# Moving the value spreads, the table load and the last store in a transfer-bound softmax kernel

## The chip, the cores and the metric

The kernel runs on one core of a Trainium2 chip. The metric is the time of one execution on the device, in microseconds (us), and a kernel's figure is the median of its runs. Ratios are the mean time of one kernel's runs over the mean of the other's runs of the same rounds, with a 95% interval, so they are not quite the ratio of the medians quoted beside them.

A trace gives the *span*, which is 1.7 to 2.4 us shorter than the run's time. Engines are PE (matrix products), PEld (its weight loads), DVE (vector), ACT (scalar), POOL and SP. A "q" behind an engine's name (SPq, ACTq) is its instruction queue. Here SP issues every load and store.

## The reference

```python
def setup_inputs():
    scores = np.random.randn(8, 12, 1024, 1024).astype(np.float32)
    v      = np.random.randn(8, 12, 1024, 64).astype(np.float32)

def reference(scores, v):
    attn = np.exp(scores - np.max(scores, axis=-1, keepdims=True))
    attn = attn / (np.sum(attn, axis=-1, keepdims=True) + 1e-8)
    return np.matmul(attn, v).astype(np.float32)
```

Seen by the kernel, these are 96 independent heads, each with 4.194 MB of scores, 0.262 MB of values and 0.262 MB of output.

## The kernel before

A loop of 24 passes takes four heads each. For a head, ACT takes the exponential of 8 rows of scores in four instructions. (A "row" is one of a head's eight tiles of 128 x 1024 scores.) PE transposes a row in eight blocks, DVE copies the transposed row out of PSUM, and PE multiplies it with `vones`, the head's values beside a column of ones whose product is the row's sum. DVE then takes the reciprocal and multiplies (the normalisation). Below, *the last product* is the last of these multiplications on DVE, not one on PE. The maximum isn't subtracted, since the scores are small.

The values of four heads come as one block of 1.049 MB, and POOL casts them to half precision. DVE then *spreads* them, in four copies a head, from their compact layout into `vones`. A store carries two heads (0.524 MB).

```python
def heads(n0):
    for k in range(AHEAD):                      # four heads of a pass
        if k == 0:
            for s in range(S):
                spread_v(k, s)                  # head 0: its own values, at the start
        st = dict(vones=vones_bufs[k])
        for r in range(R):                      # 8 rows
            ...                                 # exp (ACT), 8 transposes (PE)
            copy = nc.vector.tensor_copy(out=pt[:], in_=psT[:])
            if k < AHEAD - 1 and r % (R // S) == 0:
                spread_v(k + 1, r // (R // S), copy)   # the next head's values
            if r == R - 1:
                load_next(k, n0)                # heads 0 and 1 of the next pass
            pending.append((n0, k, r, pt, st))
            if len(pending) > LAG:
                finish(pending.pop(0))          # products, normalise, store of heads 0 and 1
    while pending:
        finish(pending.pop(0))
    cast_v()                                    # POOL: the next pass's four heads of values
    last(n0)

def last(n0):
    before = queued[-1:]
    with tc.If(n0 < BH - 2 * AHEAD) as cmp:
        ...                                     # loads of heads 2 and 3, values, store
    with cmp.Else():
        with tc.If(n0 < BH - AHEAD) as cmp2:
            ...
            load(AHEAD - 2, BH - 2, (4, 4))     # the very last heads come in pieces
            load(AHEAD - 1, BH - 1, (4,))
            store(n0, AHEAD - T)
            load(AHEAD - 1, BH - 1, (2, 1, 1), 4)
        with cmp2.Else():
            ...
            store(n0, AHEAD - T)                # the very last store, whole
```

Of the kernel before, what the change touches and what calls it, by code (L numbers as in the profile page):

```python
# [9 lines left out]
FP16 = mybir.dt.float16  # L10
EXP = mybir.ActivationFunctionType.Exp
# [3 lines left out]
def kernel(  # L15
# [7 lines left out]
    P = 128  # L23
# [52 lines left out]
    def buffers(pool, count, shape, dtype, name):  # L76
        return [pool.tile(shape, dtype, name=f"{name}{k}") for k in range(count)]

    s_bufs = buffers(sb_pool, AHEAD, [P, R, SK], FP32, "s_nat")
    v_sb = sb_pool.tile([P, C // L, S, L, D], FP32, name="v_sb")  # L80
    v_half = sb_pool.tile([P, C // L, S, L, D], FP16, name="v_half")
    p_bufs = buffers(sb_pool, 8, [P, EB, SK], FP16, "p_nat")
    pt_bufs = buffers(sb_pool, 4, [P, SK], FP16, "pt")
    out_bufs = buffers(sb_pool, 2, [P, T, R, D], FP32, "out_sb")
# [16 lines left out]
    def after(a, b):  # L101

        tc.add_manual_dep(
            a.ins,
            b.ins.name,
            mybir.DependencyInfo(mybir.DependencyClass.NoSync, mybir.DependencyReason.DATA),
            reason="order",
        )

    def queue(dma):  # L110

        if queued:
            after(dma, queued[-1])
        queued.append(dma)
# [21 lines left out]
    def finish(u):  # L136

        n0, k, r, pt, st = u
        b, g = r // G, r % G
        if r == 0:  # L140
            st["recip"] = take(rc_bufs)
            st["out_sb"] = out_bufs[k // T]
        bank = psO_whole[:, b] if k % 2 == 0 else psO_banks[b][:, 0]
        for c in range(C):
            nc.tensor.matmul(  # L145
                out=bank[:, g * M : (g + 1) * M],
                lhsT=pt[:, c * P : (c + 1) * P],
                rhs=st["vones"][:, c, 0:M],
                start=(c == 0),
                stop=(c == C - 1),  # L150
            )
        if k % 2 == 1:
            if g == G - 1:
                normalise(k, st, b, b + 1)
        elif r == R - 1:
            normalise(k, st, 0, R // G)
        if r == R - 1 and k == T - 1:
            store(n0, 0)

    def store(n0, k):  # L160

        rows = out_bh.rearrange("(m x) y -> m x y", x=P)
        dma = nc.sync.dma_start(
            out=rows[bass.ds((n0 + k) // T, 1)].rearrange("o x y -> (o x) y"),
            in_=out_bufs[k // T][:].rearrange("x t r d -> x (t r d)"),
        )
        for other in stores:
            apart(dma, other)
            apart(other, dma)
        apart(dma, dma)  # L170
        stores.append(dma)
        queue(dma)

    stores = []

    def apart(dma, other):
        tc.declare_no_dep(
            dma.ins, other.ins, across_iterations=True, reason="stores of two heads are disjoint"
        )
# [12 lines left out]
    def load_v(n):  # L192

        rows = v_bh.rearrange("(m x) y -> m x y", x=P)
        queue(
            nc.sync.dma_start(  # L196
                out=v_sb[:].rearrange("x h s l d -> x (h s l d)"),
                in_=rows[bass.ds(n // AHEAD, 1)].rearrange("o x y -> (o x) y"),
            )
        )  # L200

    def cast_v():
        nc.gpsimd.tensor_copy(out=v_half[:], in_=v_sb[:])  # L203

    def spread_v(k, s, behind=None):

        copy = nc.vector.tensor_copy(  # L207
            out=vones_bufs[k][s * Q : (s + 1) * Q, :, 0:D].rearrange(
                "i (h l) d -> i h l d", l=L
            ),  # L210
            in_=v_half[k * Q : (k + 1) * Q, :, s],
        )
        if behind is not None:
            after(copy, behind)
# [6 lines left out]
# [6 lines that stand above are left out]
            queued[:] = before  # L227
            load(AHEAD - 2, (n0 + (2 * AHEAD - 2)) % BH)
            load_v((n0 + 2 * AHEAD) % BH)
            load(AHEAD - 1, (n0 + (2 * AHEAD - 1)) % BH)  # L230
# [3 lines that stand above are left out]
                queued[:] = before  # L234
                load(AHEAD - 2, BH - 2, (4, 4))
                load(AHEAD - 1, BH - 1, (4,))
                store(n0, AHEAD - T)
                load(AHEAD - 1, BH - 1, (2, 1, 1), 4)
            with cmp2.Else():
                queued[:] = before  # L240
                store(n0, AHEAD - T)

    def heads(n0):

        for k in range(AHEAD):
            if k == 0:
                for s in range(S):
                    spread_v(k, s)
            st = dict(vones=vones_bufs[k])
            for r in range(R):  # L250
                if r % EB == 0:
                    p_nat = take(p_bufs)
                    rows = 1 if k == AHEAD - 1 and r == R - EB else EB
                    for g in range(0, EB, rows):
                        nc.scalar.activation(  # L255
                            out=p_nat[:, g : g + rows, :].rearrange(
                                "p r (x v) -> p x r v", v=Q * L
                            ),
                            in_=s_bufs[k][:, r + g : r + g + rows, :].rearrange(
                                "p r (i x l) -> p x (r i) l", i=Q, l=L  # L260
                            ),
                            func=EXP,
                        )
                p_row = p_nat[:, r % EB, :].rearrange("p (h q l) -> p h l q", q=P, l=L)
                psT = take(psT_bufs)
                for c in range(C):
                    nc.tensor.transpose(  # L267
                        out=psT[:, c * P : (c + 1) * P],
                        in_=p_row[:, c // L, c % L, :],
                        identity=order16[:],  # L270
                    )
                pt = take(pt_bufs)
                copy = nc.vector.tensor_copy(out=pt[:], in_=psT[:])  # L273
                if k < AHEAD - 1 and r % (R // S) == 0:
                    spread_v(k + 1, r // (R // S), copy)
                if r == R - 1:
                    load_next(k, n0)
                pending.append((n0, k, r, pt, st))
                if len(pending) > LAG:
                    finish(pending.pop(0))  # L280
        while pending:
            finish(pending.pop(0))
        cast_v()
        last(n0)

    assert BH % AHEAD == 0 and BH >= 2 * AHEAD and SK == Q * S * C
    load_v(0)
    for k in range(AHEAD):
        load(k, k)
    cast_v()  # L290
    load_v(AHEAD)
    with tc.For_i(0, BH, AHEAD, iteration_sync="reg_based") as n0:  # L292
        queued.clear()
# [31 lines left out]
```

## Time and profile before

| | before |
|---|---|
| time, median of the first 3 runs (range) | 1066.09 us (1065.76 to 1066.24) |
| span of the profiled run | 1064.0 us |
| busiest engine over the span | DVE, 74% |
| DMA queue busy | 99.2% of the span |
| mean pass (2 to 16), moved bytes per second | 43.67 us, 432 GB/s |
| last head: first exp to end of the last product | 13.23 us |
| end of the last product to the end | 4.81 us |

The prediction below shows the lines that carry this reading. Three more groups of the page are the ones that the change moves: the table load, the spreads and the cast. The columns are busy us, mean ns of one, and, behind the second bar, the idle time of the engine just before them and what ended most of it.

```profile
L255 ACT ACT_TABLE_LOAD x24 | 30.8, 1283 | 89.8 <-DMA s_nat<-in_scores_dram 81.7
L207 DVE COPY vones<-v_half 32x512 f16<-32x512 f16 x384 | 109.4, 285 | 22.8 <-POOL v_half L203 6.0
L203 POOL CAST v_half<-v_sb 128x2048 f16<-128x2048 f32 x25 | 47.4, 1896 | 1002.3 <-DVE vones L207 957.1
```

ACT idles 89.8 us ahead of its table loads, nearly all of it until scores land. So a table load starts only when the scores are there and stands between their landing and the exp. POOL's cast waits for DVE's spreads, as it overwrites what they read. One pass on ACT's timeline (start, duration, group, and the idle time before it):

```profile
758.44 1.28 ACT L255 ACT_TABLE_LOAD   x1 [3.56 <-DMA s_nat<-in_scores_dram]
759.73 7.32 ACT L255 ACTIVATE p_nat<-s_nat 128x2048 f16<-128x2048 f32 x4
768.12 7.32 ACT L255 ACTIVATE p_nat<-s_nat 128x2048 f16<-128x2048 f32 x4 [1.07 <-SPq L226]
779.03 7.32 ACT L255 ACTIVATE p_nat<-s_nat 128x2048 f16<-128x2048 f32 x4 [3.58 <-DMA s_nat<-in_scores_dram]
```

A head's exps take 7.32 us and its landing interval is about 10.9 us, so ACT idles more than 3 us a head. The table load of 1.28 us is paid from that idle time.

### The profile page before, as it was taken

How to read it: one execution, taken by the hardware profiler on the slowest of the kernel's cores; microseconds unless marked ns; L12 is line 12 of the kernel's file. 1: busy time of each engine (PE TensorE's matmuls, PEld its weight loads, DVE VectorE, ACT ScalarE, POOL GpSimd, SP SyncE). 2: the span in 40 equal slices, each digit the busy share in tenths (PEclk: the TensorE clock that was granted, in tenths of full speed). 3: DMA queues.
4: the chain of work that ended last, by engine and by line, in shares of the span. 5: the costliest groups of instructions: out<-in, count | busy, mean ns of one | idle time of the engine just before them, and what ended most of it. 6: DMA issues, size and time to landing. Idle time of an engine off the chain costs nothing.

```text
span 1064.0 us, 32161 instructions
## 1 busy us (share of the span) xinstructions
PE 731.4 (69%) x12288; PEld 678.4 (64%) x12288; DVE 786.6 (74%) x1589; ACT 735.6 (69%) x432; POOL 48.1 (5%) x31
## 2 busy tenths in 40 slices
PE   2766766767766677677686776867666777666676
PEld 2665756667666667666575665767565666666675
DVE  3776876868768777677786776868768687687777
ACT  3766776666767668586676866667766668676685
POOL 0000000000000000000000000000000000000000
PEclk9888888878889888888988888888889788898989
DMA  9999999999999999999999999999999999999995
GB/s 397 431 418 434 426 433 434 433 434 432 432 434 432 425 443 430 429 431 428 433 431 436 432 434 434 431 434 424 441 427 434 432 426 435 432 432 428 440 425 236
DMA packets 24772, 453.06 MB, mean 426 GB/s; under 512 B 2752, under 2 KB 2752, under 8 KB 9152
## 3 DMA queue, kind: packets, MB, share of 16 engines
q1 hardware_dynamic: 24768, 453.00, 99.2%
q8 instruction: 4, 0.07, 0.0%
HBM read 436.21 MB, written 25.17 MB: 434 GB/s over the span
## 4 chain that ended last, share of the span: by engine, by line
DMA 81%; ACT 12%; issue 3%; ACTq 1%; PE 1%; DVE 0%; SPq 0%; PEld 0%; DVEq 0%
DMA s_nat<-in_scores_dram 81%; ACT p_nat L255 12%; PE psT L267 1%; ACTq L255 1%; ACTq L226 0%; ACTq L292 0%; PE psO L145 0%; DVE pt L273 0%; PE psO_whole L145 0%; SPq L184 0%; PEld L267 0%; ACTq L320 0%; DVE out_sb L129 0%; SPq L196 0%; PEld L145 0%
## 5 line engine op out<-in xcount | busy, mean ns | idle before, releaser
L255 ACT ACTIVATE p_nat<-s_nat 128x2048 f16<-128x2048 f32 (+1 forms) x408 | 704.8, 1799 | 228.1 <-DMA s_nat<-in_scores_dram 202.2
L267 PE MATMUL psT<-order,p_nat 128*128 128x128 f16 x6144 | 574.9, 246 | 269.9 <-ACT p_nat L255 263.9
L273 DVE COPY pt<-psT 128x1024 f16<-128x1024 f16 x768 | 515.8, 687 | 200.6 <-PE L267 109.4
L267 PEld LDWEIGHTS <-p_nat 128*128 128x128 f16 x6144 | 446.5, 123 | 298.3 <-ACT p_nat L255 295.7
L145 PEld LDWEIGHTS <-pt 128*128 128x128 f16 x6144 | 302.9, 107 | 81.0 <-DVE pt L273 77.7
L145 PE MATMUL psO<-vones,pt 128*128 128x65 f16 x3072 | 177.4, 201 | 53.9 <-DVE pt L273 50.2
L145 PE MATMUL psO_whole<-vones,pt 128*128 128x65 f16 x3072 | 189.9, 211 | 2.7 <-DVE pt L273 2.4
L207 DVE COPY vones<-v_half 32x512 f16<-32x512 f16 x384 | 109.4, 285 | 22.8 <-POOL v_half L203 6.0
L255 ACT ACT_TABLE_LOAD x24 | 30.8, 1283 | 89.8 <-DMA s_nat<-in_scores_dram 81.7
L203 POOL CAST v_half<-v_sb 128x2048 f16<-128x2048 f32 x25 | 47.4, 1896 | 1002.3 <-DVE vones L207 957.1
L129 DVE TENSOR_TENSOR out_sb<-psO,recip 64x256 f32<-64x256 f32 x192 | 81.1, 423 | 6.1
L129 DVE TENSOR_TENSOR out_sb<-psO_whole,recip 64x512 f32<-64x512 f32 x96 | 66.1, 688 | 3.0
L124 DVE RECIPROCAL recip<-psO 128x4 f32<-128x4 f32 x96 | 17.1, 178 | 34.4 <-PE psO L145 17.6
L124 DVE RECIPROCAL recip<-psO_whole 128x8 f32<-128x8 f32 x48 | 9.7, 203 | 4.5 <-PE psT L267 3.9
L71 DVE MEMSET vones<- 128x16 f16 x4 | 0.2, 72 | 0.8 <-PEq L309 0.8
L62 DVE CAST order<-ident 128x128 f16<-128x128 f32 x1 | 0.2, 227 | 0.4 <-POOL ident masks.py:199 0.4
masks.py:199 POOL TENSOR_SCALAR_AFFINE_SELECT ident<-ident 128x128 f32<-128x128 f32 x1 | 0.3, 295 | 0.1
masks.py:197 POOL MEMSET ident<- 128x128 f32 x1 | 0.2, 205 | 0.3 <-POOLq L309 0.3
L309 POOL MEMSET const-float32-0.0<- 128x1 f32 x1 | 0.1, 100 | 0.2 <-issue 0.2
L309 POOL MEMSET const-bfloat16-1.0<- 128x1 bf16 x1 | 0.1, 103 | 0.0
L309 POOL MEMSET const-uint8-127<- 128x1 uint8 x1 | 0.1, 103 | 0.0
L309 POOL MEMSET const-float32-1.0<- 128x1 f32 x1 | 0.1, 100 | 0.0
## 6 DMA issues: line engine op xcount, KB each, us to landing
s_nat<-in_scores_dram SPq DMA_DIRECT2D x96, 4096.0 KB, 35.8
v_sb<-in_v_dram SPq DMA_DIRECT2D x24, 1024.0 KB, 33.1
out_dram<-out_sb SPq DMA_DIRECT2D x48, 512.0 KB, 26.9
s_nat<-in_scores_dram SPq DMA_DIRECT2D x3, 2048.0 KB, 32.4
s_nat<-in_scores_dram SPq DMA_DIRECT2D x1, 1024.0 KB, 25.4
s_nat<-in_scores_dram SPq DMA_DIRECT2D x2, 512.0 KB
```

The source lines that it names most:

```text
L62: nc.vector.tensor_copy(out=order16[:].rearrange("p (t j) -> p t j", t=T), in_=ident32[:].rearrange("p (j t) -> p t j", t=T),)
L71: nc.vector.memset(vo[:, :, D : D + 2], 1.0)
L124: nc.vector.reciprocal(out=recip, in_=psO[:, :, :, D : D + 1])
L129: nc.vector.tensor_tensor(out=rows.rearrange("j (b g) d -> j b g d", g=G), in0=psO[part, :, :, 0:D], in1=recip[part].to_broadcast([W, last ...
L145: nc.tensor.matmul(out=bank[:, g * M : (g + 1) * M], lhsT=pt[:, c * P : (c + 1) * P], rhs=st["vones"][:, c, 0:M], start=(c == 0), stop=(c ...
L203: nc.gpsimd.tensor_copy(out=v_half[:], in_=v_sb[:])
L207: copy = nc.vector.tensor_copy(out=vones_bufs[k][s * Q : (s + 1) * Q, :, 0:D].rearrange("i (h l) d -> i h l d", l=L), in_=v_half[k * Q : ( ...
L255: nc.scalar.activation(out=p_nat[:, g : g + rows, :].rearrange("p r (x v) -> p x r v", v=Q * L), in_=s_bufs[k][:, r + g : r + g + rows, :] ...
L267: nc.tensor.transpose(out=psT[:, c * P : (c + 1) * P], in_=p_row[:, c // L, c % L, :], identity=order16[:],)
L273: copy = nc.vector.tensor_copy(out=pt[:], in_=psT[:])
L309: nc = _bacc.Bacc("TRN2", target_bir_lowering=False, num_devices=1)
```

## The change

It has three parts. The spreads of heads 2 and 3 go among the copies of heads 0 and 1. Those of the *next* pass's heads 0 and 1 stand in a branch ahead of the last head, skipped in the last pass; the cast moves forward to make that possible. A dummy exp ahead of heads 0 and 3 lets the table be loaded in idle time. The very last store goes out in two halves.

```diff
-    def store(n0, k):
+    def store(n0, k, parts=1):
...                                  # one issue for each part of T * R * D columns
-                store(n0, AHEAD - T)
+                store(n0, AHEAD - T, T)
...
-            if k == 0:
-                for s in range(S):
-                    spread_v(k, s)
+            if k == AHEAD - 1:
+                with tc.If(n0 < BH - AHEAD):
+                    for part in range(2 * S):
+                        spread_v(part // S, part % S)
+            if k % (AHEAD - 1) == 0:
+                table = nc.scalar.activation(out=spare[:], in_=order16[:, 0:1], func=EXP)
...
+                        if k % (AHEAD - 1) == 0 and r == g == 0:
+                            after(exp, table)
...
-                if k < AHEAD - 1 and r % (R // S) == 0:
-                    spread_v(k + 1, r // (R // S), copy)
+                if k < 2 and r % 2 == 0:
+                    spread_v(k + 2, r // 2, copy)
...
+            if k == 1:
+                cast_v()
         while pending:
             finish(pending.pop(0))
-        cast_v()
         last(n0)
...                                  # ahead of the loop, heads 0 and 1 are spread once
```

More of the change, by code (lines that the diff above doesn't have):

```diff
@@ L81 @@
     v_half = sb_pool.tile([P, C // L, S, L, D], FP16, name="v_half")
+    spare = sb_pool.tile([P, 1], FP16, name="spare")
     p_bufs = buffers(sb_pool, 8, [P, EB, SK], FP16, "p_nat")
@@ L158, in finish @@
             store(n0, 0)
-    def store(n0, k):
+    def store(n0, k, parts=1):
         rows = out_bh.rearrange("(m x) y -> m x y", x=P)
-        dma = nc.sync.dma_start(
-            out=rows[bass.ds((n0 + k) // T, 1)].rearrange("o x y -> (o x) y"),
-            in_=out_bufs[k // T][:].rearrange("x t r d -> x (t r d)"),
-        )
-        for other in stores:
-            apart(dma, other)
-            apart(other, dma)
-        apart(dma, dma)
-        stores.append(dma)
-        queue(dma)
+        size = T * R * D // parts
+        for part in range(0, T * R * D, size):
+            dma = nc.sync.dma_start(
+                out=rows[bass.ds((n0 + k) // T, 1)].rearrange("o x y -> (o x) y")[
+                    :, part : part + size
+                ],
+                in_=out_bufs[k // T][:].rearrange("x t r d -> x (t r d)")[:, part : part + size],
+            )
+            for other in stores:
+                apart(dma, other)
+                apart(other, dma)
+            apart(dma, dma)
+            stores.append(dma)
+            queue(dma)
     stores = []
@@ L254, in heads @@
                     for g in range(0, EB, rows):
-                        nc.scalar.activation(
+                        exp = nc.scalar.activation(
                             out=p_nat[:, g : g + rows, :].rearrange(
@@ L280, in heads @@
                     finish(pending.pop(0))
+            if k == 1:
+                cast_v()
         while pending:
             finish(pending.pop(0))
-        cast_v()
         last(n0)
+    assert AHEAD == S == 4 and R == 2 * S
     assert BH % AHEAD == 0 and BH >= 2 * AHEAD and SK == Q * S * C
@@ L290 @@
     cast_v()
+    for k in range(2):
+        for part in range(S):
+            spread_v(k, part)
     load_v(AHEAD)
```

## The prediction

> **What bounds the kernel now.** I read the page's busy shares first, then its DMA lines and its table of DMA issues, then the windows of single passes, and last the timeline of the tail. The page:
>
> ```profile
> PE 731.4 (69%) x12288; PEld 678.4 (64%) x12288; DVE 786.6 (74%) x1589; ACT 735.6 (69%) x432; POOL 48.1 (5%) x31
> ...
> DMA  9999999999999999999999999999999999999995
> ...
> q1 hardware_dynamic: 24768, 453.00, 99.2%
> ...
> DMA s_nat<-in_scores_dram 81%; ACT p_nat L255 12%; PE psT L267 1%; ACTq L255 1%; ACTq L226 0%; ACTq L292 0%; PE psO L145 0%; DVE pt L273 0%; PE psO_whole L145 0%; SPq L184 0%; PEld L267 0%; ACTq L320 0%; DVE out_sb L129 0%; SPq L196 0%; PEld L145 0%
> ...
> s_nat<-in_scores_dram SPq DMA_DIRECT2D x96, 4096.0 KB, 35.8
> ```
>
> No compute engine is above 74%, while the DMA row reads 9 in every slice but the last, and its queue is busy 99.2% of the span. The last line says how deep the queue is: a 4 MB load needs 35.8 us from issue to landing. At 432 GB/s its own 4.19 MB take 9.7 us, so some three and a half loads stand in the queue when it is issued. Two whole passes of four heads (a row: stretch, length, busy us of PE, PEld, DVE, ACT, POOL, then the clock, the DMA share and GB/s):
>
> ```profile
> 487.03:530.70 43.67, 30.63 (x512) 28.25 (x512) 32.72 (x66) 30.68 (x19) 1.90 (x1) 0.85 1.01 432
> 530.70:574.37 43.67, 30.71 (x512) 28.62 (x512) 32.80 (x66) 30.63 (x19) 1.90 (x1) 0.85 1.01 432
> ```
>
> A pass loads four heads of 4.194 MB, one block of values of 1.049 MB, and stores two blocks of 0.524 MB: 18.87 MB, and 18.87 MB / 432 GB/s = 43.7 us, the period itself. The busiest engine, DVE, has 32.8 us of work in it, 10.9 us less. So 23 of 24 passes are paid for by bytes, and the change moves the same bytes.
>
> What is not paid for by bytes is the two ends. The start is about 2 us. The tail, from the landing of the last head's first four rows (1045.86, in the chain of waits in order of time) to 1064.0, is 18.1 us. Its timeline, ACT and DVE and the last store's issue:
>
> ```profile
> 1045.96 7.59 ACT L255 ACTIVATE p_nat<-s_nat 128x2048 f16<-128x2048 f32 x5 [1.14 <-DMA s_nat<-in_scores_dram]
> ...
> 1051.03 0.69 DVE L273 COPY pt<-psT 128x1024 f16<-128x1024 f16 x1
> ...
> 1051.76 1.41 DVE L129 TENSOR_TENSOR out_sb<-psO_whole,recip 64x512 f32<-64x512 f32 x2
> ...
> 1052.56 7.02 SPq L163 DMA_DIRECT2D out_dram<-out_sb  x2
> ...
> 1053.20 1.89 DVE L273 COPY pt<-psT 128x1024 f16<-128x1024 f16 x3
> ...
> 1055.78 0.88 DVE L129 TENSOR_TENSOR out_sb<-psO,recip 64x256 f32<-64x256 f32 x2
> ...
> 1056.69 0.69 DVE L273 COPY pt<-psT 128x1024 f16<-128x1024 f16 x1
> ...
> 1058.31 0.88 DVE L129 TENSOR_TENSOR out_sb<-psO,recip 64x256 f32<-64x256 f32 x2
> ```
>
> ACT ends its last row at 1053.55, but DVE copies that row's transposed scores only at 1056.69: in the tail DVE is the limit, without a pause from 1050.8 to 1057.4. The last product ends at 1059.19, the store goes out at 1059.22, and its bytes move here:
>
> ```profile
> 1059.50:1060.00 0.50, 0.00 (x0) 0.00 (x0) 0.00 (x0) 0.00 (x0) 0.00 (x0) 0.50 0.00 0
> 1060.00:1060.50 0.50, 0.00 (x0) 0.00 (x0) 0.00 (x0) 0.00 (x0) 0.00 (x0) 0.50 0.90 360
> 1060.50:1061.00 0.50, 0.00 (x0) 0.00 (x0) 0.00 (x0) 0.00 (x0) 0.00 (x0) 0.50 0.99 410
> 1061.00:1061.50 0.50, 0.00 (x0) 0.00 (x0) 0.00 (x0) 0.00 (x0) 0.00 (x0) 0.50 0.67 270
> ```
>
> That is 0.8 us from issue to first byte, 1.35 us of bytes (0.52 MB), and 2.6 us from there to the end in which nothing moves.
>
> **What the Trainium skill says.** "DMA: Bandwidth & Descriptors", section "Where 436 GB/s comes from", derives a ceiling of 435.2 GB/s from the 16 SBUF ports; this trace's passes run at 431 to 432, within 1% of it. The same section calls about 358 GB/s the binding limit of HBM transfers per core; this trace is above that, so the measurement decides. Section "Latency and other measured facts" gives about 0.6 us to the first byte on the path that SP issues on; here it is 0.8. "ScalarE: Activation LUTs", section "What ACT_TABLE_LOAD costs", has 1283 ns for a table load plus 1380 ns of drain; the page has 24 loads of 1283 ns, and the exp behind one starts within 10 ns (496.34 + 1.28 = 497.62 against 497.63), so no drain of that size shows here. "Advanced Engine Details and Errata", section "Control Flow Timing", has 108 ns for a compare-and-branch and 51 for an unconditional one; in the chain of waits a branch on ACT takes about 0.33 us with its issue gaps.
>
> **The change part by part.** The order of instructions shows where each part lands.
>
> First, the spreads. A pass still has 16 copies of 0.285 us on DVE. Those of heads 2 and 3 go behind the copies of heads 0 and 1. Those of the next pass's heads 0 and 1 stand in a branch that DVE reaches after the second row of head 2: 8 x 0.285 = 2.3 us plus about 0.3 us of branch. Net work per pass: +0.3 us of 32.8, against a period of 43.7. The normalisation behind the branch, hence the store and the load of head 2 that SP issues after it, go out some 2.5 us later, against a queue of about 35 us: worth 0. The cast of the values on POOL moves ahead of head 2, so the load of values no longer waits for it (97.3 us in 23 waits of the queue before): it goes out earlier into a full queue, worth 0.
>
> In the last pass the branch is skipped. Heads 2 and 3 then have no spreads. Before, head 2 had four among its copies (the last at 1042.78, 1045.27, 1046.91 and 1048.55), about 4 x 0.3 = 1.2 us. DVE stood 4 us behind ACT there: head 2's last exp ended at 1044.82, its last copy began at 1048.87. I re-time DVE from 1042.78 without them: head 2's last copy ends at 1048.3 in place of 1049.5. From here DVE catches up with ACT, which is bound by the landing. The last head's row 2 needs the second exp (end 1049.78) and about 0.77 us to a copy (a first exp of 517.00 + 1.90 leads to a copy at 519.67), so its copy starts at 1050.55 in place of 1051.03. Everything behind it is back to back on DVE as before, so the end moves by **0.48 us** and not by 1.2.
>
> Second, the table loads. There are still 24. Each moves from behind the landing of a pass's first head to ahead of it: 1.28 us less between landing and exp, in each pass. The freed buffer is reloaded 1.28 us earlier, into the full queue: worth 0, as the next landing is set by bytes. The second dummy exp, before the last head, finds the table loaded: about 0.2 us. With the branch's 0.33 us it fits in the 1.14 us that ACT idles before 1045.96: also 0.
>
> Third, the last store. The first half needs only the first of the two last products, 0.44 us ahead of the second. Its issue (0.36 us) and its 0.26 MB then lie before or beside the second half's. Before, the bytes end 2.25 us after the last product (1061.45 against 1059.19). Now: product end to second issue 0.03, first byte 0.8, bytes 0.65 and about 0.2 of the first half still ahead of it: 1.7 us. Worth **0.55 us**.
>
> Sum: 0 + 0.48 + 0.55 = 1.03 us. 1066.09 - 1.03 = 1065.06, which I give as **1065.0 us**.
>
> **The rivals.** (a) The queue runs dry in the middle, because a pass boundary holds loads back, and then the earlier spreads, cast and table load shorten every pass: 23 x 1.28 us = 29 us, 2.8%, hence about 1036. For it speaks the chain of waits, which holds 12% of exps and starts each head's exp at a landing. Against it: 432 GB/s and a DMA share of 1.0 in each pass, and 35.8 us to landing. The chain alternates landing and exp only because a load is issued when its buffer is free; its landing is set by what stands before it in the queue. (b) The branch stalls DVE, as its copies wait for POOL's cast, which waits for values landing about 2.4 us behind head 2 (1.05 MB at 432 GB/s), at about the time DVE gets there. A stall of 2 us per pass would cost 48 us if DVE were the bound; with 10.9 us of room it costs nothing in a pass. In the last pass the branch is skipped. Time unchanged. (c) The tail is bound elsewhere: if the exps' landing or the branch delays the last head, the 0.48 goes, leaving 1065.5; if smaller rows of 2 KB in the halved store move slower, its 0.55 goes, leaving 1065.6; both, about 1066.1. (d) The tail gains all of the 1.2 us, if the last head's copies are not held up by the second exp: then 1064.3.
>
> **Range and chances.** (c) and (d) with the run spread of before (1065.76 to 1066.24) give 1064.0 to 1066.2. Faster by over 2% needs 21 us, more than the whole tail, so only (a) can bring it: 0.01. Slower by over 2% needs a starved queue: 0.01. Within 2%: 0.98.
>
> **What would show it.** Right: passes of 43.7 us at 432 GB/s with a DMA share of 1.0, while the idle time before the table load no longer ends in a landing; fewer waits of ACT behind landings but the same number of landings; in the tail no spread among head 2's copies, the last head's first exp still right at a landing near 1045.9, its row 2 copied about 0.5 us earlier, and 1.7 us from the last product to the last byte. Wrong: passes that differ in length from 43.7 us, a DMA slice under 9 in the middle, an ACT that starts the last head after its landing, or a tail that shrinks by more than 1.5 us.

## The result, and the profile after

| | before | after |
|---|---|---|
| time, median of 4 runs each (range) | 1065.92 us (1065.48 to 1066.24) | 1066.06 us (1065.30 to 1066.19) |
| ratio | | 1.0000 [0.9983, 1.0017] |
| span of the profiled run | 1064.0 us | 1063.5 us |

The time is the same. The profile says that the change did in the middle what was foreseen. The page of the kernel after, in the same order as before:

```profile
PE 725.8 (68%) x12288; PEld 669.1 (63%) x12288; DVE 780.7 (73%) x1589; ACT 743.2 (70%) x480; POOL 48.1 (5%) x31
...
q1 hardware_dynamic: 24912, 453.00, 99.2%
...
L258 ACT ACT_TABLE_LOAD x24 | 30.8, 1283 | 1.8 <-ACTq L309 1.4
...
s_nat<-in_scores_dram SPq DMA_DIRECT2D x96, 4096.0 KB, 34.1
```

The bytes and the queue's 99.2% are those of before. The 24 table loads no longer wait for a landing: 1.8 us of idle time stand before them in all, in place of 89.8. A load now needs 34.1 us to landing in place of 35.8: it is issued later, but still far ahead.

Three passes of the kernel after, each measured from the first exp of a pass's last head to that of the next pass's last head, which starts at a landing in both kernels (a row as in the prediction: stretch, length, busy us of PE, PEld, DVE, ACT, POOL, then clock, DMA share, GB/s):

```profile
485.26:528.92 43.66, 30.84 (x512) 28.49 (x512) 32.88 (x67) 30.96 (x21) 1.89 (x1) 0.84 1.01 432
747.45:791.25 43.80, 30.71 (x512) 28.34 (x512) 32.60 (x66) 30.95 (x20) 1.89 (x1) 0.84 1.00 431
791.25:835.04 43.79, 30.26 (x512) 27.59 (x512) 32.40 (x66) 30.96 (x20) 1.89 (x1) 0.88 1.00 431
```

The last two of these passes in the kernel before:

```profile
747.47:791.19 43.72, 29.55 (x512) 27.16 (x512) 32.80 (x66) 30.65 (x19) 1.98 (x2) 0.88 1.00 431
791.19:834.87 43.68, 30.76 (x512) 28.74 (x512) 32.73 (x66) 30.64 (x18) 1.55 (x2) 0.84 1.01 432
```

The engines have the same work, and the rate differs by 1 GB/s at most, but the later passes of the kernel after are about a tenth of a us longer. One pass is no evidence for so little, as passes of the kernel before vary from 43.60 to 43.72; many together are. These are the same marks, the first exp of the last head of a pass, from the timelines of ACT:

```
last head of pass        2        16        23      2 to 16   16 to 23
before                92.40    703.78   1009.58      611.38     305.80
after                 92.19    703.63   1010.04      611.44     306.41
```

For fourteen passes the kernels run alike, and over the next seven the kernel after loses 0.61 us. Now the tail of the kernel after, ACT and DVE (start, duration, group, idle time):

```profile
1046.61 7.65 ACT L265 ACTIVATE p_nat<-s_nat 128x2048 f16<-128x2048 f32 x5 [1.02 <-DMA s_nat<-in_scores_dram]
...
1051.27 0.69 DVE L285 COPY pt<-psT 128x1024 f16<-128x1024 f16 x1 [0.21 <-PE L279]
...
1056.92 0.69 DVE L285 COPY pt<-psT 128x1024 f16<-128x1024 f16 x1
...
1058.55 0.87 DVE L130 TENSOR_TENSOR out_sb<-psO,recip 64x256 f32<-64x256 f32 x2
```

The last head's first exp starts at its landing, but at 1046.61 in place of 1045.96. Its row 2 is copied 4.66 us behind that start (1051.27), where it was 5.07 us before (1051.03 - 1045.96): the tail itself is faster. And the last store's bytes, the last product having ended at 1059.42:

```profile
1059.50:1060.00 0.50, 0.00 (x0) 0.00 (x0) 0.00 (x0) 0.00 (x0) 0.00 (x0) 0.50 0.25 98
1060.00:1060.50 0.50, 0.00 (x0) 0.00 (x0) 0.00 (x0) 0.00 (x0) 0.00 (x0) 0.50 1.01 389
1060.50:1061.00 0.50, 0.00 (x0) 0.00 (x0) 0.00 (x0) 0.00 (x0) 0.00 (x0) 0.50 1.00 385
1061.00:1061.50 0.50, 0.00 (x0) 0.00 (x0) 0.00 (x0) 0.00 (x0) 0.00 (x0) 0.50 0.46 176
```

They end about 1.8 us behind the last product; before it was 2.25.

From here on each trace is split in three: the *stream*, from the start to the last head's first exp; from there to the *end of the last product*; and from there to the *end*.

| us | stream | exp to last product | product to end | span |
|---|---|---|---|---|
| before | 1045.96 | 13.23 | 4.81 | 1064.0 |
| after | 1046.61 | 12.81 | 4.08 | 1063.5 |

One profile of each can't say more. The runs of one kernel differ by up to 0.9 us, and both the +0.65 in the stream and the -0.73 behind the product could be chance. Three theories were open. *First theory*: the stream's difference is chance, and the tail's gain of about 1 us is real. *Second theory*: the change slows the stream and so gives back what the tail gains. *Third theory*: the tail's gain is an accident of one profile.

### The profile page after: what moved, and what is told of

It reads as the page before. It is cut to its first block, busy times and chain, and to the rows that moved or that the text cites. A ratio compares the mean times of both kernels' runs of the same rounds, so it can differ in the third digit from the quotient of the medians.

```text
span 1063.5 us, 32373 instructions
## 1 busy us (share of the span) xinstructions
PE 725.8 (68%) x12288; PEld 669.1 (63%) x12288; DVE 780.7 (73%) x1589; ACT 743.2 (70%) x480; POOL 48.1 (5%) x31
## 3 DMA queue, kind: packets, MB, share of 16 engines
q1 hardware_dynamic: 24912, 453.00, 99.2%
## 5 line engine op out<-in xcount | busy, mean ns | idle before, releaser
L279 PE MATMUL psT<-order,p_nat 128*128 128x128 f16 x6144 | 556.7, 243 | 231.2 <-ACT p_nat L265 224.7
L279 PEld LDWEIGHTS <-p_nat 128*128 128x128 f16 x6144 | 437.8, 122 | 255.2 <-ACT p_nat L265 252.5
L146 PEld LDWEIGHTS <-pt 128*128 128x128 f16 x6144 | 296.9, 107 | 133.6 <-DVE pt L285 128.1
L146 PE MATMUL psO<-vones,pt 128*128 128x65 f16 x3072 | 183.6, 203 | 58.5 <-DVE pt L285 56.6
L146 PE MATMUL psO_whole<-vones,pt 128*128 128x65 f16 x3072 | 186.1, 209 | 42.6 <-DVE pt L285 42.6
L258 ACT ACT_TABLE_LOAD x24 | 30.8, 1283 | 1.8 <-ACTq L309 1.4
L258 ACT ACTIVATE spare<-order 128x1 f16<-128x1 f16 x48 | 9.5, 198 | 0.3
## 6 DMA issues: line engine op xcount, KB each, us to landing
s_nat<-in_scores_dram SPq DMA_DIRECT2D x96, 4096.0 KB, 34.1
```

The source lines that it names most:

```text
L146: nc.tensor.matmul(out=bank[:, g * M : (g + 1) * M], lhsT=pt[:, c * P : (c + 1) * P], rhs=st["vones"][:, c, 0:M], start=(c == 0), stop=(c ...
L258: table = nc.scalar.activation(out=spare[:], in_=order16[:, 0:1], func=EXP)
L279: nc.tensor.transpose(out=psT[:, c * P : (c + 1) * P], in_=p_row[:, c // L, c % L, :], identity=order16[:],)
```

## The experiments

Each kernel ran in rounds beside the kernel before on the same chip, and each was profiled once. "Before" in the text is the median of the same session. All outputs were right unless said otherwise.

### The two kernels again

No edit in either. First the kernel before:

> The kernel before, unchanged, as a control. All theories: 1065.5 to 1066.5 us. I split each trace in two: the stream, from the start to the first exp of the last head (1045.96 us before), and the tail, from there to the end (18.0 us before; 16.9 after the change). Theory 1 (the tail got shorter, and the stream varies by chance from run to run): stream anywhere from 1045.3 to 1046.9, tail 18.0 within 0.2. Theory 2 (the change itself slows the stream): stream within 0.2 of 1045.96 again. Theory 3 (the tail was an accident of one trace): tail anywhere from 16.9 to 18.0.

It took 1065.84 us against 1065.92 (ratio 0.9999 [0.9985, 1.0013], 5 rounds). Its trace: stream 1045.91, then 13.24 and 4.45. The stream and the first part of the tail agree with the first profile to 0.05 us; product to end is 0.36 shorter, so that part of the first profile was high. Then the kernel after:

> The changed kernel again. Theory 1: tail 16.9 within 0.2, stream 1045.3 to 1046.9 and not tied to the kernel, so the time is about 1 us below before in the mean of many runs. Theory 2: tail 16.9, stream 1046.6 within 0.2 with passes of 43.8 us in the last third again, time equal to before. Theory 3: tail between 16.9 and 18.0.

1066.19 us (1065.54 to 1066.95) against 1065.92, ratio 1.0004 [0.9990, 1.0018]. Its trace: stream 1046.84, then 13.08 and 4.08. The stream is late again, by about 0.9 us, which speaks against chance. The 4.08 is there again too.

### The last store in halves, alone, and the change without it

Alone on the kernel before:

```diff
-                store(n0, AHEAD - T)
+                store(n0, AHEAD - T, T)      # the very last store only
...                                  # and store() with parts, as in the change
```

> The kernel before with only the last store in halves. Theory 1: from the last product's end to the end of the trace 0.5 to 0.7 us less than before (4.8 before, 4.1 after), while the last product still ends 13.2 us after the last head's first exp starts; tail 17.4. Theory 3: no difference from before in the tail. Theory 2 (if the halves had anything to do with the stream, which I doubt): stream 1046.6.

1065.78 us against 1065.92 (0.9999 [0.9985, 1.0013]): the medians can't tell it. The trace can: product to end 4.09 us. Its stream was 1046.30, longer than the other traces of the kernel before; 0.35 us of that come from a single pass of 44.02 us, in which one of the DMA engines fell behind once (two packets at 792 us took 1.41 and 1.55 us, where 1.21 is usual).

The reverse, on the kernel after, is the same line put back to the whole store:

```diff
-                store(n0, AHEAD - T, T)
+                store(n0, AHEAD - T)
```

> The changed kernel with its last store whole. Theory 1: the last product ends 12.8 us after the last head's first exp starts, as in the changed kernel (13.2 before), and the end follows 4.8 us later as before; tail 17.6, stream by chance. Theory 2: stream 1046.6 within 0.2, tail 17.6, time 0.5 us above before. Theory 3: tail as in before.

1066.02 us against 1065.92 (1.0003 [0.9989, 1.0017]). Product to end is 4.54 and the first part of the tail 12.82, as in the kernel after. The stream is 1046.64, late again. So the halves have nothing to do with the stream, and they are worth about 0.47 us: 4.55 with a whole store, the mean of six traces of all those told of here (4.44 to 4.81; the run with wrong results left out), against 4.08 in four with halves (4.06 to 4.09; three more, whose tail is changed otherwise too, have 4.24, 4.07 and 4.06). The third theory falls, and the first now has three late streams out of three against it.

### Which part slows the stream

The second theory now had two variants: the dummy exps and the earlier table load (2a), or the moved spreads with their cast and branch (2b). The table load alone, on the kernel before:

```diff
+            if k == 0:
+                table = nc.scalar.activation(out=spare[:], in_=order16[:, 0:1], func=EXP)
...
+                        if k == 0 and r == g == 0:
+                            after(exp, table)
```

> The kernel before with only the table load moved to idle time, by a dummy exp ahead of each pass's first head. In four traces so far the stream (start to the last head's first exp) was 1045.9, 1045.9 and 1046.3 us without the moved spreads and table loads, and 1046.6, 1046.8, 1046.6 with them, where six to nine passes of the last ten took 43.8 us in place of 43.7. Theory 2a (the earlier exps of the first head, hence the earlier table load, slow the stream): stream 1046.6 within 0.2, passes of 43.8 us appear. Theory 2b (the spreads and what goes with them do it): stream 1045.9 within 0.3, no pass at 43.8. Theory 1 (chance): either. In all, the first head's exp starts 1.28 us earlier in each pass, the tail is 18.0 within 0.3 and the time 1065.5 to 1066.8.

1065.91 us against 1066.15 (0.9999 [0.9983, 1.0016]); stream 1045.96, then 13.22 and 4.52. This is the kernel before to a tenth, so 2a falls, as far as one trace of each can say (the dummy exp ahead of head 3 isn't in this run; the next one has neither). It also shows that the table load is worth nothing, as predicted.

The moved spreads, cast and branch alone, which is the kernel after without the dummy exps and with the last store whole:

```diff
-            if k % (AHEAD - 1) == 0:
-                table = nc.scalar.activation(out=spare[:], in_=order16[:, 0:1], func=EXP)
...
-                store(n0, AHEAD - T, T)
+                store(n0, AHEAD - T)
```

> The kernel before with only the spreads and the cast moved (the branch), without the dummy exps and with the last store whole. Theory 2a: stream 1045.9 within 0.3, no passes of 43.8. Theory 2b: stream 1046.6 within 0.2, passes of 43.8 in the last third. Theory 1: either. In all: last product 12.8 us after the last head's first exp, as with the whole change; time 1065.3 to 1066.5.

1066.57 us (1066.43 to 1067.12) against 1066.15 (1.0006 [0.9989, 1.0023]); stream 1047.21, the latest of all; then 12.75 and 4.44. So 2b holds: the moved spreads, with the cast and the branch that go with them, both shorten the tail and lengthen the stream.

What the longer stream looks like is at the landing of its last pieces. Two stretches of this kernel's tail, where the last bytes of scores come in:

```profile
1052.00:1052.50 0.50, 0.50 (x14) 0.45 (x11) 0.49 (x1) 0.50 (x1) 0.00 (x0) 1.00 0.06 25
1052.50:1053.00 0.50, 0.29 (x5) 0.11 (x2) 0.47 (x1) 0.50 (x2) 0.00 (x0) 1.00 0.06 25
```

A DMA share of 0.06 is that of one engine of sixteen (1/16 = 0.0625): I read it as fifteen with nothing left to move and one still carrying. In the kernel before, the same stretches read:

```profile
1051.50:1052.00 0.50, 0.38 (x8) 0.29 (x6) 0.47 (x2) 0.50 (x2) 0.00 (x0) 1.00 0.04 16
1052.00:1052.50 0.50, 0.50 (x17) 0.50 (x15) 0.47 (x2) 0.50 (x1) 0.00 (x0) 1.00 0.00 0
```

There everything has come by 1052.

Each transfer has sixteen completions in the trace, which I take as one for each engine, and a load has landed with the last of them. I took, for each transfer, how far each completion lies behind the median of the sixteen. (The records don't name the engine, so an engine is followed by its lag.) Twelve stay within about 0.3 us of the median. Three fall behind early and stay there. In the kernel before they are 1.3 to 1.6 us late by 58 us; the first two appear in the landings that follow 16 KB packets of another queue ("instruction" on the page), at 27.0 and 36.7 us, of about 0.95 us each, the third after one at 47.2 us. A slow spot at 63 to 65 us, just ahead of the first store, makes it 1.9 to 2.5 us. The last of the sixteen falls behind steadily (below, the *growing engine*):

```
lag behind the median, us     100-300   300-500   950-1045   latest of the three
before                          0.42      0.98      2.24       2.42
before, control                 0.45      1.07      2.18       2.40
before + halves                 0.40      1.00      2.17       2.71
before + table load             0.56      1.13      2.3        2.26
after                           0.42      1.31      2.97       2.28
after, control                  0.55      1.58      3.19       2.40
after, last store whole         0.45      1.38      2.85       2.08
spreads alone                   0.28      1.19      3.40       2.32
```

(The columns are stretches of the run in us, with the mean lag of the growing engine, and last the lag of the latest of the other three at the end.) In the kernel before, the growing engine doesn't reach the latest of the three, so the landings keep their distance and a pass stays at 43.7 us. The trace with the halves alone has the same growing engine, but one of its three is 2.71 us behind from 802 us on: that falls in the pass of 44.02 us and goes with its stream, 0.37 us later than the 1045.93 below. In the kernel after the growing engine passes the three at about 725 us, where the passes begin to be longer (in the other three traces with moved spreads between 560 and 660 us), and from there on it sets the landings. At the end it is 0.69, 0.79, 0.77 and 1.08 us behind the three in the four traces with moved spreads; their streams are 0.68, 0.91, 0.71 and 1.28 us later than 1045.93, the mean of the two plain traces of the kernel before.

The load that lets the last head start shows it most plainly:

```
completion of that load, us    median of the sixteen    last of the sixteen
before                               1043.44                  1045.86
before, control                      1043.40                  1045.81
before + table load                  1043.43                  1045.85
after                                1043.40                  1046.50
after, control                       1043.40                  1046.74
after, last store whole              1043.57                  1046.54
spreads alone                        1043.53                  1047.10
```

Most engines are done with it at the same time in all seven traces, and what is late is the last one. That is where the microsecond goes.

### A better tail

For a version that beats both, I took the kernel before, split the last head's first piece in two, and let both normalisations of the last head wait until its last row is copied; the last store goes in halves.

```diff
-                load(AHEAD - 1, BH - 1, (4,))
+                load(AHEAD - 1, BH - 1, (2, 2))
...
-            if g == G - 1:
+            if k == AHEAD - 1:
+                if r == R - 1:
+                    normalise(k, st, 0, 1)
+                    normalise(k, st, 1, 2)
+            elif g == G - 1:
                 normalise(k, st, b, b + 1)
...
-                store(n0, AHEAD - T)
+                store(n0, AHEAD - T, T)
```

> An attempt at a better version on the kernel before: last store in halves, the last head's first four rows loaded in two pieces of two rows, and the first normalisation of a pass's last head put behind its last copy. Theory 1 and 2 agree: its stream ends as before in bytes, but the first exp of the last head starts up to 1.1 us earlier, right behind the one before it; of DVE's 0.72 us idle before the last normalisation 0.7 is filled; end of trace about 1.5 to 2.3 us before 1064.0 in sum with the halves' 0.6; time 1063.5 to 1064.8.

1064.58 us (1064.40 to 1064.65) against 1066.15 (1065.64 to 1066.44). The ranges don't touch; the ratio is 0.9986 [0.9969, 1.0003], whose interval, over so few runs, just reaches 1. DVE's tail in this kernel:

```profile
1050.75 0.69 DVE L281 COPY pt<-psT 128x1024 f16<-128x1024 f16 x1
...
1055.55 0.69 DVE L281 COPY pt<-psT 128x1024 f16<-128x1024 f16 x1 [0.15 <-PE L145]
...
1056.36 0.88 DVE L129 TENSOR_TENSOR out_sb<-psO,recip 64x256 f32<-64x256 f32 x2
...
1057.48 0.88 DVE L129 TENSOR_TENSOR out_sb<-psO,recip 64x256 f32<-64x256 f32 x2
```

The last row is copied at 1055.55 in place of 1056.69. Of these 1.14 us, 0.28 were there at row 2 already (1050.75 for 1051.03), and the rest comes behind it, where no multiplication of the first half stands ahead of the last row any more. The last product ends at 1058.36 in place of 1059.19. In three parts the trace has 1044.64, 13.72 and 4.24: the last head's first exp is 1.3 us earlier, as its first two rows have landed before ACT is free, but DVE, still behind, turns only 0.28 of that into an earlier row 2. The three edits of this version weren't run one by one. The growing engine's lag is 2.17 us, as in the kernel before. This is the fastest version.

### The branch, or when the work falls

Within 2b two variants were open: the branch itself costs something that holds back issues (2c), or it is the time at which DVE spreads (2d). To take the branch away and leave the order, the eight spreads go before the normalisation of head 1 and run in every pass, the last included; the last store is whole.

```diff
+        if k == 1 and r == R - 1:
+            for part in range(2 * S):
+                spread_v(part // S, part % S)
...
-            if k == AHEAD - 1:
-                with tc.If(n0 < BH - AHEAD):
-                    for part in range(2 * S):
-                        spread_v(part // S, part % S)
```

> The changed kernel with its last store whole, the eight spreads of the next pass at the same place in DVE's order but without a branch around them (in the last pass they run too and are not used). The landings in the traces show one of the 16 DMA engines falling further behind the others in every kernel: 0.4 to 2.2 us over the run without the moved spreads, 0.4 to 3.0 with them, where it passes the three others that are 2.3 us late and then sets the landing of each load. Theory 2c (the branch brings that engine extra work): its lag ends at 2.2, stream 1045.9 within 0.3. Theory 2d (the new times of the spreads, cast and issues against the transfers do it): lag ends near 3, stream 1046.6 to 1047.2. In both, the last product ends about 14.5 us after the last head's first exp, as DVE has 2.3 us more in the last pass; time 1066.5 to 1068.

1069.83 us (1069.34 to 1070.07) against 1065.70, ratio 1.0038 [1.0021, 1.0055]: 0.4% slower, and in the tail. From first exp to last product are 16.75 us where I had expected 14.5. The last pass now does the eight useless spreads shortly before its last head:

```profile
1044.84 2.49 DVE L215 COPY vones<-v_half 32x512 f16<-32x512 f16 x8 [0.26 <-POOL v_half L211]
```

Those 2.49 us and a wait are about 2.75 of the 3.9 us that the tail is longer than in the kernel after with a whole store (16.75 - 12.82); the rest I didn't take apart. The engine's lag is 2.73 us and the stream 1046.31, between the kernels before and after. So neither variant is right alone: without a branch about half of the lateness is still there (0.38 us, where the four traces above have 0.68 to 1.28). This rests on one trace.

### Without the first store of a pass

Is the lag made by the stores? The store of heads 0 and 1 is left out in all passes but the last. The result is wrong (the outputs not written read as NaN).

```diff
-            store(n0, 0)
+            store(n0, 0, cond=n0 >= BH - AHEAD)
...                                  # store() hands the condition on to its DMA
```

> The kernel before without the store of a pass's first two heads in all passes but the last (a wrong result on purpose). If bytes set the time, as predicted: 23 x 0.524 MB = 12.06 MB less at 432 GB/s, so 27.9 us less, 1038 us, passes of 42.5 us. If a compute engine or the chain of exps set it: under 5 us less. If the slow engine's lag comes from store packets, as their lengths in the trace suggest (most of the extra time is in the 4 KB packets of stores), its lag grows by less than half as much, 0.4 to about 1.0 us; if not, to 2.2 as before.

1038.04 us against 1065.70, 27.66 us less; the estimate from the bytes was 23 x 0.524 MB / 432 GB/s = 27.9. A pass:

```profile
515.15:557.52 42.37, 29.89 (x512) 27.66 (x512) 32.74 (x66) 30.65 (x19) 1.73 (x2) 0.88 1.00 432
```

The pass is 1.3 us shorter at the same rate, with the same work on the engines: bytes set the time. And the lag doesn't grow: 0.18, 0.19 and 0.17 us in the three stretches.

The traces have each packet of a store. A 4 KB packet usually takes 155 to 159 ns. In nearly every store of heads 0 and 1, and in some of those of heads 2 and 3, a few take longer, mostly by 10 to 30 ns: before the tail at most five of 128, and nearly always one right behind the other, so I take them to be of one engine. Their time above 155 ns, summed over the run up to the tail, beside the lag at the end:

```
                              extra time of store packets, us    lag at the end, us
before / control                    1.95 / 1.74                    2.24 / 2.18
before + halves                     1.96                           2.17
before + table load                 1.94                           2.3
better tail                         1.66                           2.17
after / control                     3.13 / 3.22                    2.97 / 3.19
after, last store whole             3.01                           2.85
spreads alone                       3.51                           3.40
without the branch                  2.30                           2.73
without the first store             0                              0.17
```

The lag goes with the extra time, and where there are no slow packets the lag doesn't grow. In the first profile of the kernel before, 1.63 us of it lie in the stores of heads 0 and 1 and 0.31 in those of heads 2 and 3; in the kernel after, 2.26 and 0.87. Where the first store is left out, the second has no slow packets either, though it is unchanged. So the lag is in the stores' packets. Leaving a store out also shifts all that follows, so that it was this store, and not the shift, is argued and not shown. What slows their packets on that engine, and why that differs between kernels that store the same bytes, isn't shown.

### Twice the spreads

If the number of spreads in their new places were the cause, doubling them would double the growth of the lag. In the kernel after, each spread is done twice:

```diff
-        copy = nc.vector.tensor_copy(
+        for _ in range(2):
+            copy = nc.vector.tensor_copy(
```

> The changed kernel with every spread done twice: 16 more copies of 0.285 us, 4.6 us more of DVE per pass (37 of 43.7 us). If DVE has the room that I took it to have: passes of 43.7 us, time within 1 us of the changed kernel's 1066.1. If DVE or the spreads' place is on the path of the stream: up to 23 x 4.6 = 105 us more.

1066.69 us (1065.74 to 1066.79) against 1065.70 (1.0005 [0.9988, 1.0022]). The passes are 43.67 us (the mean from pass 2 to 16, and 43.69 from there to pass 23) and the stream is 1045.91, as in the kernel before: the lag at the end is 1.96 us, with 1.9 us of extra time in the stores, and only there does it reach the three (1.89). The tail is 2.0 us longer (14.83), since in the last pass DVE falls behind with its double spreads. So 4.6 us more of DVE work in a pass cost nothing in the pass (DVE has that room), and the loss in the stream does not go with the amount of spreading: with the branch, the early cast and twice the spreads in their new places it isn't there. What is left is when things happen (the first store of a pass, for one, is issued some 3.5 us later here than in the kernel after: 485.89 against 482.40), and no run took that apart.

### The better tail on the kernel after

The two edits of the better tail, on the kernel after:

```diff
-                load(AHEAD - 1, BH - 1, (4,))
+                load(AHEAD - 1, BH - 1, (2, 2))
...                                  # and both normalisations after the last row, as above
```

> The changed kernel with the two tail measures of the attempt before (two pieces of two rows, late first normalisation). That attempt on the kernel before took 1064.6 us. Here the last head's first exp starts as soon as ACT is free and DVE has 1.2 us less in the tail, so from the last landing to the end another 0.5 to 1.2 us less; the stream is 0.7 us later by theory 2. Time 1063.6 to 1065.0.

1065.22 us (1064.82 to 1065.48) against 1065.70 (0.9994 [0.9977, 1.0011]), just over what I had expected. The lag is 2.89 us, that of the kernel after, with 2.8 us of extra time in the stores. Its three parts are 1045.43, 13.60 and 4.07, where the better tail on the kernel before has 1044.64, 13.72 and 4.24: the moved spreads bring little further to this tail and keep their cost in the stream.

### Half of the moved spreads

If only the spreads of the next pass's heads 0 and 1 cost something, those of heads 2 and 3 could move early and spare the tail its four. On the better tail, both are put into head 1, with no branch and no moved cast:

```diff
-                if k < AHEAD - 1 and r % (R // S) == 0:
-                    spread_v(k + 1, r // (R // S), copy)
+                if k < 2 and r % 2 == 0:
+                    spread_v(k + 1, r // 2, copy)
+                if k == 1 and r % 2 == 1:
+                    spread_v(k + 2, r // 2, copy)
```

> The attempt at a better version (on the kernel before), with the spreads of heads 2 and 3 both among the copies of head 1, so that head 2 has none, without a branch and with the spreads of heads 0 and 1 where they were. If DVE's 1.2 us of spreads in head 2 are what keeps it behind in the tail: the end 0.3 to 0.8 us earlier than that attempt's 1064.6, so 1063.8 to 1064.3. If the slow engine's lag follows from when DVE, POOL and SP act against the store's bytes, it can end anywhere between 2.2 and 3 us, and 0.7 us of the gain may go; if only the moved spreads of heads 0 and 1 set it, it ends at 2.2 us.

1065.24 us (1065.11 to 1065.51) against 1066.00 (0.9991 [0.9978, 1.0005]): a miss, and slower than the better tail by itself (1064.58, on another chip). The lag at the end is 2.30 us, below the latest of the three (2.49), as that idea wanted. But the last head of the first pass already began 0.35 us later (46.08 against 45.73), and in the tail DVE now waits 0.25 to 0.27 us for PE before each of the last head's first two rows. The last product ends at 1059.54. Why is not settled.

## Why the prediction was right or wrong

**The bound** was right. Passes of both kernels are 43.67 us at 432 GB/s in the mean from pass 2 to 16 (611.38 / 14 and 611.44 / 14), leaving out 12.1 MB (23 x 0.524) saves 27.7 us, and 4.6 us more DVE work in a pass cost nothing.

**The table loads** were worth 0, as said: the idle time ahead of them went from 89.8 to 1.8 us, and alone they left everything in place. ACT's timeline of the kernel after shows where the time went:

```profile
754.88 1.28 ACT L258 ACT_TABLE_LOAD   x1
...
758.38 7.32 ACT L265 ACTIVATE p_nat<-s_nat 128x2048 f16<-128x2048 f32 x4 [2.00 <-PE L146]
768.04 7.32 ACT L265 ACTIVATE p_nat<-s_nat 128x2048 f16<-128x2048 f32 x4 [2.35 <-SPq L231]
779.17 7.32 ACT L265 ACTIVATE p_nat<-s_nat 128x2048 f16<-128x2048 f32 x4 [3.80 <-DMA s_nat<-in_scores_dram]
```

The table load now comes behind the previous head with no wait. The first head's exp starts 1.35 us earlier (758.38 for 759.73), but the idle time stands in front of it, 2.00 us, and of the second head, 2.35 us for 1.07. The third head's exp, for 779.03, is at 779.17. It starts when its scores land, whatever came before. Rival (a), shorter passes, is dead.

**The tail's spreads** were predicted at 0.48 us. From the first exp to the last product it is 13.25 us in four traces without moved spreads (before, control, halves, table load: 13.22 to 13.31) and 12.87 in four with them (after, control, whole store, spreads alone: 12.75 to 13.08): 0.39 us.

**The halved store** was predicted at 0.55 us and measured at 0.47 (4.55 - 4.08).

**The step that failed** is in the first part of the change, the store, the loads and the values that are issued later or earlier, "worth 0" both, "as the next landing is set by bytes", in the prediction's words on the table load. The argument behind it was that a full queue doesn't care when an entry joins, and it holds for the queue's depth: it never ran dry. But the price isn't a gap in the queue. The last head's first exp comes at 1046.03 in the four traces without moved spreads (1045.91 to 1046.30) and at 1046.83 in the four with them (1046.61 to 1047.21): **+0.80 us**. So the sum is not 0 - 0.48 - 0.55 = -1.03 but, as measured, 0.80 - 0.39 - 0.47 = -0.06 us, and that is what the runs show. The prediction took the mean rate of sixteen engines, which is the same in both kernels within 1 GB/s, for the time of a landing. A landing is set by the slowest engine, and in the kernel after the slowest is one whose store packets got slower. The predicted sign "the last head's first exp still right at a landing near 1045.9" was the right one to watch: it starts at a landing, but one that comes 0.7 us late. In the terms of the rivals, part of (c) came true, a delayed landing, by a cause that it didn't name; its other part, slower halves of the store, didn't, and neither did (d). The range reached up to 1066.2 for rival (c); that the measured 1066.06 lies in it is luck more than foresight, since the loss came by another way. (Its own sum was 1065.06, which it rounded down to 1065.0.)

**Rival (b)**, a branch that stalls DVE for POOL's cast, is there in the first pass and costs nothing. DVE and SP in the kernel after:

```profile
50.29 2.49 DVE L212 COPY vones<-v_half 32x512 f16<-32x512 f16 x8 [9.40 <-POOL v_half L208]
```

```profile
54.51 0.36 SPq L166 DMA_DIRECT2D out_dram<-out_sb  x1
55.45 0.35 SPq L189 DMA_DIRECT2D s_nat<-in_scores_dram  x1
```

DVE waits 9.40 us there, and the first store and the load of head 2 behind it are issued at 54.51 and 55.45, where the kernel before issued them at 43.15 and 44.10. Yet the last head of the second pass starts, at its landing, at 92.19, against 92.40 before: more than 11 us of delay are absorbed by the depth of the queue. In the later pass that I looked at (521.37), DVE reaches the branch without a wait.

**Open**: what makes a few store packets on one engine 10 to 30 ns slower, and why that differs between these kernels, which move the same bytes. When the spreads, the cast and the issues fall is what is left of the differences, but no run shows that it is the cause. The branch by itself and the number of spreads are excluded as the whole cause; the rest is not known. The streams were compared on single profiles, four to a side, whose ranges don't touch (the run without the branch, 1046.31, and that with twice the spreads, 1045.91, are told above and not counted in); the run times alone, with ranges of 0.5 to 1.4 us, couldn't have shown it.

## What to carry to other kernels

In a kernel bound by transfers as this one is, only the two ends can be won by moving work, and what is won there can be lost again in the stream. So split each trace at the last landing, and compare the parts and not the totals. A load lands with its slowest DMA engine: look at the spread of the completions over the engines, and at a share of 1/16 at the end of a stream, and don't trust the mean rate. In the tail, let the work that the last row needs go first and normalise later; with smaller first pieces and the halved store, that gave the version whose runs all lay below those of both kernels.

## What the Trainium skill lacked or had wrong

- "DMA: Bandwidth & Descriptors", section "Latency and other measured facts", says that engines 7 and 15 are usually slower and ties that, as a best guess, to the rings of transfers issued by GpSimd's software. Here all loads and stores are issued by SP, and still one engine loses 0.09 us a pass (before: 2.2 us over 24 passes) to store packets of 4 KB that take mostly 10 to 30 ns longer than their 155 to 159 ns; three others sit 1.9 to 2.4 us behind after the first 70 us. No run here shows which physical engines these are.
- No page that I read explains why some 4 KB packets of a store are slow: their sum went from 1.95 to 3.13 us as DVE's spreads and the cast moved, to 1.9 with the spreads there done twice, and to 0 when nearly half of the stores were left out. Whether the compute engines' timing does it isn't shown.
- "ScalarE: Activation LUTs", section "What ACT_TABLE_LOAD costs", adds 1380 ns of drain to the 1283 of the load. The prediction found 10 ns behind the load. The kernel after has the other side as well: a load at 1017.48 comes 0.03 us behind an exp that ended at 1017.45, and a dummy exp starts at 1018.77. No drain of that size stands on either side. The page speaks of a switch to a different set of functions; this kernel's ACT computes exp alone, and what the page doesn't say is whether a load without such a switch drains too.
